# Streaming Conformer layer on one core: the last loads of x are tied behind weight casts, and 19 products by g move from GpSimd to VectorE

## The chip, the cores and the metric

The kernel runs on one core of one Trainium2 chip. The time is device microseconds of that core for one execution. The engines are TensorE (PE in the profile; PEld its weight loads), VectorE (DVE), ScalarE (ACT), GpSimd (POOL) and SyncE (SP), which here only starts transfers.

## The reference, cut to what matters

One layer is computed for 512 prompt frames and 64 sample frames (576 rows in all, width 2048). What the change touches is its end:

```python
mix = jnp.concatenate([conv_out * jax.nn.silu(cg), att * jax.nn.silu(ag), mem * jax.nn.silu(mg)], axis=-1)
y = layer_norm(ALPHA * x + mix @ w_out, ln_g, ln_b)
def layer_norm(x, g, b):
    mu = jnp.mean(xf, axis=-1, keepdims=True)
    var = jnp.mean(jnp.square(xf - mu), axis=-1, keepdims=True)
    return (xf - mu) * lax.rsqrt(var + LN_EPS) * g + b
```

All inputs are float32. The attention and memory half of `mix @ w_out` is finished earlier and waits in DRAM (`a_dram`); what is left for the end is the convolution half, of depth 1024.

## The kernel before, in words

**Weights.** A weight tile of 128x1024 is loaded by SP (`wraw`, line 175), or summed by a GpSimd transfer that adds to what is there (`w_add`, line 179). It is split in two: ScalarE casts it to the high part `whi` (line 248), VectorE subtracts that and gives the low part `wlo` (line 253). TensorE multiplies high by high, high by low and low by high. A pair `whi`, `wlo` is called a stage here; `next_stage` asks for it, and splits up to two stages ahead. All of `wraw`, `wsum`, `whi` and `wlo` share 14 buffers (`NW`), so a load or a cast also waits until the last reader of its buffer is done.

**The end of the kernel.** The output has four blocks of 512 columns, n = 0 to 3, and five row tiles, t = 0 to 4 (t = 4 are the 64 sample rows). Blocks 0 and 1 are computed together by `out_pair(0, ...)`, a scheme of seven products with two stages each: B11, T1, T2, B21, T3, B22 and T4 (stages 0 to 13), on TensorE in lines 1121 to 1127. The scheduler may reorder them: four matmuls of T2 and all of T3 wait for `t23l` of the last depth tile (line 1078), whose buffer is that of `xd`, and so TensorE does B22 and the `xd` matmuls of T4 (lines 1125 and 1127) ahead of them. Block 2 is a plain product of four stages (`tileB`, lines 343 to 349), block 3 another, written out in `part` row tile by row tile (lines 1405 to 1410).

**The tiles z.** z[t, n] holds ALPHA * x plus the attention half, then the sum with the convolution half. `load_z` starts the load of x on ScalarE's queue (line 1172); `form_z` scales it on ScalarE (line 1180) and starts a GpSimd transfer that adds `a_dram` to it (line 1181). For n = 2 and 3 `next_z(2)` does two tiles of each at a time, from stage 11 of `out_pair` on. VectorE adds the accumulators (lines 1361 and 1334) and takes statistics (lines 1366 and 1335); GpSimd multiplies z by g (lines 1367, 1337 and 1425; line 1430 does the last one on VectorE). `finish_stats` makes mean and rstd on GpSimd (lines 1300 to 1310), and `finish_pe` transposes them, lets TensorE form g times minus mean times rstd plus b (line 1323), and VectorE makes y (line 1326), which SP stores.

**Order.** A scheduler places the instructions of each engine by the order in the code and by its own estimate of when they can start; each engine then runs its list strictly in order. `tc.issue_after(ins)` makes the instructions of its block that run on the engine of `ins` stand behind `ins`.

Of the kernel before, what the change touches and what calls it, by code (L numbers as in the profile page):

```python
# [9 lines left out]
F32 = mybir.dt.float32  # L10
# [5 lines left out]
P = 128  # L16
NP_TOK = 512
NS_TOK = 64
# [110 lines left out]
def hymba_kernel(ctx: ExitStack, tc: tile.TileContext, wst, xT, memT, xp, xs, kcT, vc, mkcT, mvc, biasx,  # L129
                 cconvT, convw, convb, clg, clb, lngb, sel,  # L130
                 y_out, conv_out, kT_out, v_out, mkT_out, mv_out):
    nc = tc.nc
# [35 lines left out]
        return dpool.tile(shape, F32, tag=name, name=name)  # L168

    wraw, whi, wlo, sum3 = {}, {}, {}, {}  # L170

    def w_fetch(b):
        if b not in wraw:
            wraw[b] = wtile("wraw")
            nc.sync.dma_start(wraw[b], wst[where[b]])
        return wraw[b]
# [6 lines left out]
    def w_load(i):  # L183
        if i >= len(plan):
            return
        it = plan[i]
        if it[0] == "O":
            q = out_quads(*it[1:4])
            for b in item_blocks(it):
                w_fetch(b)  # L190
            if it in added:
                return
            added.add(it)
            if it[4] == "s1":
                w_add(w_fetch(q["a21"]), q["a22"])
            elif it[4] == "s3":
                sum3[it[1:4]] = wtile("wsum")
                nc.scalar.copy(sum3[it[1:4]], w_fetch(q["a11"]))
                w_add(sum3[it[1:4]], q["a21"])
            elif it[4] == "s4":  # L200
                w_add(w_fetch(q["a21"]), q["a12"])
            return
        for b in item_blocks(plan[i]):
            w_fetch(b)
        if plan[i][2:] == ("s1",) and plan[i][1] not in sum3:
            n = plan[i][1]
            q = quads(PAIRS[n])
            sum3[n] = wtile("wsum")
            nc.scalar.copy(sum3[n], w_fetch(q["a11"]))  # L209
            w_add(sum3[n], q["a21"])  # L210
            if n != 1:
                w_add(w_fetch(q["a21"]), q["a22"])

    def w_source(it):
        if it[0] == "P":
            return w_fetch(it[1])
        if it[0] == "O":
            q = out_quads(*it[1:4])
            if it[4][0] == "a":
                return w_fetch(q[it[4]])  # L220
            if it[4] == "s3":
                return sum3[it[1:4]]
            a21 = w_fetch(q["a21"])
            if it[4] == "s2":
                nc.vector.tensor_add(a21, a21, w_fetch(q["a11"]))
            return a21
        n, form = it[1:]
        q = quads(PAIRS[n])
        if form[0] == "a":
            return w_fetch(q[form])  # L230
        if form == "s3":
            return sum3[n]
        a21 = w_fetch(q["a21"])
        if form != "s1" or n == 1:
            nc.vector.tensor_add(a21, a21, w_fetch(q[{"s1": "a22", "s2": "a11", "s4": "a12"}[form]]))
        return a21
# [6 lines left out]
    def w_split(i):  # L243
        if i < len(plan) and i not in whi:
            w_load(i)
            src = w_source(plan[i])
            hi, lo = wtile("whi", F32R), wtile("wlo", F32R)
            nc.scalar.copy(hi, src)  # L248
            if by_transfer(i):
                nc.scalar.mul(lo, hi.bitcast(F32), -1.0)  # L250
                w_add(lo, plan[i][1])
            else:
                nc.vector.tensor_sub(lo, src, hi.bitcast(F32))  # L253
            whi[i], wlo[i] = hi, lo

    def weights(i):
# [63 lines left out]
    def tileB(lhs, tiles, sample, klist, ntaps=0, before=None, early=False, steps=2):  # L320
        accs = [bank("accB") for _ in tiles]
        sacc = bank("accS") if sample else None
        nk = len(klist)
        for s in range(nk // 2):
            if before:
                before(s)
            hi, lo = next_stage()
            for kk in range(2):
                ki = 2 * s + kk
                k = klist[ki]  # L330
                ws = slice(kk * 512, (kk + 1) * 512)
                st, en = ki == 0, ki == nk - 1
                if early and st:
                    for t, acc in zip(tiles, accs):
                        nc.tensor.matmul(acc, lhs(k, t)[0], hi[:, ws], start=True, stop=False)
                    for t, acc in zip(tiles, accs):
                        nc.tensor.matmul(acc, lhs(k, t)[0], lo[:, ws], start=False, stop=False)
                    for t, acc in zip(tiles, accs):
                        nc.tensor.matmul(acc, lhs(k, t)[1], hi[:, ws], start=False, stop=False)
                else:  # L340
                    for t, acc in zip(tiles, accs):
                        lh, ll = lhs(k, t)
                        nc.tensor.matmul(acc, lh, hi[:, ws], start=st, stop=False)  # L343
                        nc.tensor.matmul(acc, ll, hi[:, ws], start=False, stop=False)  # L344
                        nc.tensor.matmul(acc, lh, lo[:, ws], start=False, stop=en)  # L345
                if sample:
                    ss = sample(k)
                    nc.tensor.matmul(sacc, ss, hi[:, ws], start=st, stop=False)
                    nc.tensor.matmul(sacc, ss, lo[:, ws], start=False, stop=en)
            pump(ntaps, steps)  # L350
        return accs, sacc
# [810 lines left out]
    z = {}  # L1162

    zload = deque()

    def load_z(n, tiles=range(5)):

        for t in tiles:
            rows = P if t < 4 else NS_TOK
            ns = slice(n * 512, (n + 1) * 512)  # L1170
            z[t, n] = t5([P, 512], "z")
            nc.scalar.dma_start(z[t, n][:rows], xp[t * P:(t + 1) * P, ns] if t < 4 else xs[:, ns])
            zload.append((t, n))

    def form_z(count):

        for _ in range(min(count, len(zload))):
            t, n = zload.popleft()
            zt = z[t, n][:P if t < 4 else NS_TOK]
            nc.scalar.mul(zt, zt, ALPHA)  # L1180
            nc.gpsimd.dma_start(zt, a_dram[t, n][:P if t < 4 else NS_TOK], accum_op=ALU.add)
# [79 lines left out]
    for j in range(NCB):  # L1261
        if j + 3 < NCB:
            load_cg(j + 3)
        acc = tileA(srhs, 1)
# [17 lines left out]
    for n in range(4):  # L1282
        raw = t6([5, 512], "gbraw")
        nc.sync.dma_start(raw, lngb[:, n * 512:(n + 1) * 512])
        hi = t6([5, 512], "gbhi", F32R)
# [6 lines left out]
    def load_g(n):  # L1292
        g = t6([P, 512], "gb")
        nc.gpsimd.dma_start(g, lngb[0:1, n * 512:(n + 1) * 512].to_broadcast((P, 512)))
        return g
# [32 lines left out]
            return last  # L1328
        return [lambda n=n: apply(n)() for n in range(4)]

    def settle(t, n, acc, g, scaled=True):
        rows = P if t < 4 else NS_TOK
        zt = z[t, n][:rows]
        nc.vector.tensor_add(zt, out_source(t, acc), zt)
        nc.vector.bn_stats(stats[t][:rows, n], zt)
        if scaled:
            nc.gpsimd.tensor_mul(zt, zt, g[:rows])

    gpair = [load_g(n) for n in range(2)]

# [3 lines left out]

    ztiles = [(t, n) for n in (2, 3) for t in range(5)]

    def next_z(count):
        form_z(count)
        for _ in range(min(count, len(ztiles))):
            t, n = ztiles.pop(0)  # L1350
            load_z(n, (t,))

    def conv_forms(stage):
        if stage < 4:
            form234(stage, alloc_large)
        elif stage >= 11:
            next_z(2)

    def zsum(t, n, acc, op=None):
        zt = z[t, n][:P if t < 4 else NS_TOK]  # L1360
# [2 lines left out]
    def done(t, n):  # L1363
        rows = P if t < 4 else NS_TOK
        zt = z[t, n][:rows]
        nc.vector.bn_stats(stats[t][:rows, n], zt)
        nc.gpsimd.tensor_mul(zt, zt, gpair[n][:rows])

    def zsink(h, n, last, op=None):
        def f(acc):  # L1370
# [6 lines left out]
    def zsample(i, acc):  # L1377
# [5 lines left out]
    out_pair(0, {"p1": zsink(0, 0, False), "p5": zsink(1, 1, False, sub), "p16": zsink(1, 0, False),  # L1383
                 "p2": zsink(0, 0, True), "p167": zsink(1, 1, True, sub), "p53": zsink(1, 0, True),
                 "p1674": zsink(0, 1, True, sub), "sample": zsample}, conv_forms)
    g = load_g(2)
    accs, sacc = tileB(mlhs2, range(4), msl, list(range(8)), before=lambda s: next_z(2))
    while zload:
        next_z(2)
    g3 = load_g(3)  # L1390
    for t in range(4):
        settle(t, 2, accs[t], g)
    settle(4, 2, sacc, g)
    g = g3
    accs = [bank("accB") for _ in range(5)]

    def part(t, s, w):
# [16 lines left out]
    for t in (4, 0, 1, 2, 3):  # L1414
        todo = []
        for s in range(4):
            part(t, s, held[s])
            if due and (t > 0 and s == 3 and t < 4 or t == 1 and s == 2):
                todo += finish_pe(*due.pop(0))
        settle(t, 3, accs[t], g, False)  # L1420
        aggr, *rest = finish_stats(t)
        due.append((t, *rest))
        rows = P if t < 4 else NS_TOK
        if t != 3:
            nc.gpsimd.tensor_mul(z[t, 3][:rows], z[t, 3][:rows], g[:rows])
        with tc.issue_after(aggr.ins):
            for f in todo:
                f()
            if t == 3:
                nc.vector.tensor_mul(z[t, 3][:rows], z[t, 3][:rows], g[:rows])  # L1430
    for d in due:
        for f in finish_pe(*d):
            f()
# [69 lines left out]
```

## Time and profile before

| what | value |
|---|---|
| median of 3 runs | 954.44 us (950.99, 954.44, 955.18) |
| profiled execution, its own time | 950.69 us |
| its span, first to last instruction | 948.4 us |
| TensorE busy | 924.8 us, 98% of the span |
| VectorE busy | 740.7 us, 78% |
| ScalarE busy | 479.4 us, 51% |
| GpSimd busy | 149.5 us, 16% |

Each row group further down says which view it is from. A timeline row gives the start, the busy time, engine, line, operation and tiles; xN merges N like instructions, and the bracket at its end is the idle time of the engine ahead of it, and what ended it. Successive matmuls overlap in the record, so the step from one start to the next is the cost of one, not its duration.

### The profile page before, as it was taken

Reading aid. Unit: us, or ns where it says so; the run is one execution under the profiler, and the core shown is the slowest. Engines: PE = TensorE matmul, PEld = TensorE weight load, DVE = VectorE, ACT = ScalarE, POOL = GpSimd, SP = SyncE. Lnnn points to the kernel's source line nnn. Section 1 sums busy time; section 2 is a strip of 40 time slices with the busy share of each in tenths; the row PEclk is TensorE's granted clock in tenths of the full one; section 3 lists DMA queues with packets and bytes.
Section 4 is the critical chain, followed back from the end, with each engine's and each line's share of the span. In section 5 each row is a group of like instructions: output and inputs, shape, how many; then the busy total and the mean of one; then the engine's idle time right before and its main releaser. Section 6 shows DMA issues by size and latency. Waiting matters only on the chain. (4 is left out here: it accounts for less than half of the span.)

```text
span 948.4 us, 15430 instructions
## 1 busy us (share of the span) xinstructions
PE 924.8 (98%) x5965; PEld 852.3 (90%) x5965; DVE 740.7 (78%) x1072; ACT 479.4 (51%) x805; POOL 149.5 (16%) x217
## 2 busy tenths in 40 slices
PE   8999999999999999999999999999999999987996
PEld 5899999999999999999999988999888799965874
DVE  7878985997699699677999565279987886746766
ACT  6655444445444544464643556447756675533200
POOL 0020000100100110011110000200112212224452
PEclk9999999999999999999999999999999999997998
DMA  9746555655666766589867456974669688896305
GB/s 327 216 148 172 146 152 157 200 148 147 185 167 181 201 181 161 176 243 231 199 182 183 144 170 210 254 167 98 153 239 248 187 291 208 199 229 165 105 1 199
DMA packets 61771, 174.74 MB, mean 184 GB/s; under 512 B 7678, under 2 KB 12286, under 8 KB 61698
## 3 DMA queue, kind: packets, MB, share of 16 engines
q1 hardware_dynamic: 38834, 106.90, 34.2%
q0 software_dynamic: 16640, 54.62, 28.6%
q10 hardware_dynamic: 6224, 12.24, 3.8%
q8 instruction: 46, 0.75, 0.3%
q14 instruction: 27, 0.22, 0.1%
HBM read 150.40 MB, written 23.33 MB: 183 GB/s over the span
## 5 line engine op out<-in xcount | busy, mean ns | idle before, releaser
L248 ACT CAST whi<-wraw 128x1024 fp32r<-128x1024 f32 x195 | 203.6, 1049 | 177.2 <-PE st L559 51.4
L253 DVE TENSOR_TENSOR wlo<-wraw,whi 128x1024 fp32r<-128x1024 f32 x173 | 217.3, 1259 | 74.9 <-ACT whi L248 37.2
L559 PE MATMUL st<-x,whi 128*128 128x288 f32 x1024 | 204.6, 294 | 0.0
L519 DVE SCALAR_TENSOR_TENSOR acc<-up,cw_sb,acc 128x606 f32<-128x606 f32 x232 | 196.3, 846 | 4.2
L559 PEld LDWEIGHTS st<-x,whi 128*128 128x128 f32 x1024 | 164.0, 188 | 0.3 <-ACT neg L628 0.2
L559 PE MATMUL st<-x,wlo 128*128 128x288 f32 x512 | 150.8, 295 | 0.0
L315 PE MATMUL accA<-x,whi 128*128 128x288 f32 x768 | 134.9, 297 | 0.0
L315 PEld LDWEIGHTS accA<-x,whi 128*128 128x128 f32 x768 | 112.7, 189 | 1.6 <-issue 0.8
L559 PEld LDWEIGHTS st<-x,wlo 128*128 128x128 f32 x512 | 96.0, 188 | 0.0
L315 PE MATMUL accA<-x,wlo 128*128 128x288 f32 x384 | 82.2, 296 | 0.0
L559 PE MATMUL st<-t13h,wlo 128*128 128x288 f32 x256 | 75.5, 295 | 0.0
L559 PE MATMUL st<-t13l,whi 128*128 128x288 f32 x256 | 75.4, 295 | 0.0
L559 PE MATMUL st<-t13h,whi 128*128 128x288 f32 x256 | 75.4, 294 | 0.0
L1121 PE MATMUL ob<-whi,mix 128*128 128x512 f32 x176 | 58.0, 411 | 7.1 <-ACT whi L248 7.1
L315 PEld LDWEIGHTS accA<-x,wlo 128*128 128x128 f32 x384 | 61.8, 189 | 0.0
L179 POOL DMA_DIRECT2D wsum<-in_wst_dram x22 | 20.9, 950 | 216.8 <-ACT wsum L209 127.8
L559 PE MATMUL st<-t,whi 128*128 128x288 f32 x256 | 51.3, 295 | 0.0
L179 POOL DMA_DIRECT2D wraw<-in_wst_dram x27 | 27.0, 1012 | 137.7 <-DVE pos L615 57.4
L559 PEld LDWEIGHTS st<-t13h,whi 128*128 128x128 f32 x256 | 48.0, 188 | 0.0
L559 PEld LDWEIGHTS st<-t13l,whi 128*128 128x128 f32 x256 | 48.0, 188 | 0.0
L559 PEld LDWEIGHTS st<-t13h,wlo 128*128 128x128 f32 x256 | 48.0, 188 | 0.0
L1121 PEld LDWEIGHTS ob<-whi,mix 128*128 128x128 f32 x176 | 34.3, 199 | 15.0 <-ACT whi L248 7.9
(391 smaller groups left out, 1855.1 us busy)
## 6 DMA issues: line engine op xcount, KB each, us to landing
wraw<-in_wst_dram SPq DMA_DIRECT2D x151, 512.0 KB, 3.9
wraw<-in_wst_dram POOLq DMA_DIRECT2D x27, 512.0 KB, 7.2
wsum<-in_wst_dram POOLq DMA_DIRECT2D x22, 512.0 KB, 6.4
wlo<-in_wst_dram POOLq DMA_DIRECT2D x22, 512.0 KB, 7.6
xraw<-in_xT_dram SPq DMA_DIRECT2D x19, 288.0 KB, 5.9
ad<-c POOLq DMA_DIRECT2D x16, 256.0 KB, 5.1
z<-in_xp_dram ACTq DMA_DIRECT2D x16, 256.0 KB, 4.9
z<-ad POOLq DMA_DIRECT2D x16, 256.0 KB, 6.4
```

The costliest lines, as they stand in the source:

```text
L179: nc.gpsimd.dma_start(dst, wst[where[b]], accum_op=ALU.add)
L248: nc.scalar.copy(hi, src)
L253: nc.vector.tensor_sub(lo, src, hi.bitcast(F32))
L315: nc.tensor.matmul(acc[:, :HALF], stat[:, ws], mv[:, c], start=ki == 0 and pi == 0, stop=ki == len(klist) - 1 and pi == 2)
L519: nc.vector.scalar_tensor_tensor(acc[0], up[0][:, t:t + ACCW], cw_sb[:, j, t:t + 1], acc[0], op0=ALU.mult, op1=ALU.add)
L559: nc.tensor.matmul(acc[:, :HALF], stat[:, ws], mv, start=first and k == 0 and i == 0, stop=k == 7 and i == 2, skip_group_check=not first)
L1121: nc.tensor.matmul(a, stat[:, os_], mv[:, ws], start=first and ki == 0 and i == 0, stop=ki == 3 and i == 2, skip_group_check=not first)
```

## The change

It has three parts. `newest` remembers the last traced cast of a high part, and the last subtraction that made a low part. In `next_z` the scalings and loads of z for n = 2 and 3 stand behind the newest cast on ScalarE, and the first two calls only load, so that a scaling follows its load two calls later. The 10 products by g of blocks 0 and 1 are done on VectorE within block 2, behind low parts; the 9 others, of blocks 2 and 3, on VectorE within block 3, behind the statistics of a row tile. The diff, cut where it only renames:

```diff
@@ w_split @@
-            nc.scalar.copy(hi, src)
+            newest["cast"] = nc.scalar.copy(hi, src).ins
...
-                nc.vector.tensor_sub(lo, src, hi.bitcast(F32))
+                newest["low"] = nc.vector.tensor_sub(lo, src, hi.bitcast(F32)).ins
@@ settle, done @@
-        if scaled:
-            nc.gpsimd.tensor_mul(zt, zt, g[:rows])
...
-        nc.gpsimd.tensor_mul(zt, zt, gpair[n][:rows])
@@ next_z @@
-    def next_z(count):
-        form_z(count)
-        for _ in range(min(count, len(ztiles))):
-            t, n = ztiles.pop(0)
-            load_z(n, (t,))
+    def next_z(stage):
+        with tc.issue_after(newest["cast"]):
+            if stage > 1:
+                form_z(2)
+            for _ in range(min(2, len(ztiles))):
+                t, n = ztiles.pop(0)
+                load_z(n, (t,))
@@ conv_forms @@
         elif stage >= 11:
-            next_z(2)
+            next_z(stage - 11)
@@ block 2 @@
-    accs, sacc = tileB(mlhs2, range(4), msl, list(range(8)), before=lambda s: next_z(2))
-    while zload:
-        next_z(2)
+    def block2(s):
+        next_z(3 + s)
+        with tc.issue_after(newest["low"]):
+            for t, n in scale_g[3 * s:3 * s + 3]:
+                rows = P if t < 4 else NS_TOK
+                nc.vector.tensor_mul(z[t, n][:rows], z[t, n][:rows], gpair[n][:rows])
+    scale_g = [(t, n) for n in range(2) for t in range(5)]
+    accs, sacc = tileB(mlhs2, range(4), msl, list(range(8)), before=block2)
@@ block 3 @@
-        if t != 3:
-            nc.gpsimd.tensor_mul(z[t, 3][:rows], z[t, 3][:rows], g[:rows])
         with tc.issue_after(aggr.ins):
             for f in todo:
                 f()
-            if t == 3:
-                nc.vector.tensor_mul(z[t, 3][:rows], z[t, 3][:rows], g[:rows])
+            for u, n, g in [(t, 3, g3)] + [(u, 2, g2) for u in {4: (4, 0), 0: (1, 2, 3)}.get(t, ())]:
+                rows = P if u < 4 else NS_TOK
+                nc.vector.tensor_mul(z[u, n][:rows], z[u, n][:rows], g[:rows])
```

On ScalarE, from the high part of T2's second stage (`whi_9062`) on, this stood before; `whi_9084` and `whi_9101` are B21, `whi_9122` and `whi_9142` T3, `whi_9176` (in the changed kernel 9173) the first stage of B22, and the tiles z are those of blocks 2 and 3:

```order
L248 CAST whi_9062<-wraw_8832 128x1024 [waits PE_49]
L1172 DMA z_9238<-in_xp_dram 128x512 [waits DVE_49]
L1180 ACTIVATE z_9236<-z_9236 128x512 [waits DMAHW6_49]
L248 CAST whi_9084<-wraw_8983 128x1024 [waits DMAHW4_49,PE_49]
L1172 DMA z_9268<-in_xp_dram 128x512 [waits DMAHW0_49]
L1180 ACTIVATE z_9238<-z_9238 128x512 [waits DMAHW7_49]
L1172 DMA z_9270<-in_xp_dram 128x512 [waits DVE_49]
L248 CAST whi_9101<-wraw_9027 128x1024 [waits DMAHW5_49,DVE_49]
L1180 ACTIVATE z_9268<-z_9268 128x512 [waits DMAHW0_49]
L248 CAST whi_9122<-wsum_8985 128x1024 [waits DMASW5_49,PE_49]
L1180 ACTIVATE z_9270<-z_9270 128x512 [waits DMAHW1_49]
L248 CAST whi_9142<-wsum_9029 128x1024 [waits DMASW7_49,PE_49]
```

In the changed kernel the same engine has, from the second stage of T3 on (`whi_9173` and `whi_9191` are B22, `whi_9213` and `whi_9235` T4, `whi_9261` the first stage of block 2):

```order
L249 CAST whi_9142<-wsum_9029 128x1024 [waits DMASW7_49,PE_49]
L249 CAST whi_9173<-wraw_8766 128x1024 [waits DMASW6_49,DVE_49]
L249 CAST whi_9191<-wraw_8832 128x1024 [waits DMASW0_49,DVE_49]
L1159 COPY ztmp_9168<-os_1310_8931 64x512 [waits PE_49]
L249 CAST whi_9213<-wraw_9146 128x1024 [waits DMAHW6_49,PE_49]
L1173 DMA z_9231<-in_xp_dram 128x512
L1173 DMA z_9233<-in_xp_dram 128x512
L249 CAST whi_9235<-wraw_9177 128x1024 [waits DMAHW7_49,DVE_49]
L1173 DMA z_9257<-in_xp_dram 128x512
L1173 DMA z_9259<-in_xp_dram 128x512
L249 CAST whi_9261<-wraw_9195 128x1024 [waits DMAHW0_49,DVE_49]
L1181 ACTIVATE z_9231<-z_9231 128x512 [waits DMAHW1_49]
```

All loads and scalings of these tiles moved behind the casts of the first stage of T4 and later ones; the nine casts from `whi_9062` to `whi_9213` follow each other with nothing of z between them.

On SP the buffers fell otherwise, so that the weight loads wait for other instructions. Before, the four loads from the first stage of T4 (`wraw_9146`) to the second of block 2 (`wraw_9222`) read as follows; the DVE wait of the first is for the low part of T3's first stage:

```order
L175 DMA wraw_9146<-in_wst_dram 128x1024 [waits DMASW5_49,DMAHW3_49,DMASW1_49,DVE_49]
L175 DMA wraw_9180<-in_wst_dram 128x1024 [waits DMAHW6_49,PE_49]
L175 DMA wraw_9198<-in_wst_dram 128x1024 [waits DMAHW7_49,PE_49]
L175 DMA wraw_9222<-in_wst_dram 128x1024 [waits DMASW0_49,DMAHW0_49,DVE_49,Activation_49]
```

and in the changed kernel, where the PE waits of the first three are for the last matmul of T2's first stage, and for the last of B21's first and of its second stage:

```order
L176 DMA wraw_9146<-in_wst_dram 128x1024 [waits DMAHW6_49,DVE_49,PE_49]
L176 DMA wraw_9177<-in_wst_dram 128x1024 [waits DMAHW7_49,DVE_49,PE_49]
L176 DMA wraw_9195<-in_wst_dram 128x1024 [waits DMAHW0_49,DVE_49,PE_49]
L176 DMA wraw_9217<-in_wst_dram 128x1024 [waits DMASW0_49,DMAHW2_49,DVE_49,Activation_49]
```

The load of T4's first stage thus no longer waits for a low part that is made late in the chain, but for a matmul of T2.

On VectorE, within block 2, the low parts stood close together before (`wlo_9432` is the first of block 3):

```order
L1361 TENSOR_TENSOR z_8611<-z_8611,ob_1309_8930 128x512 [waits PE_49]
L1366 BN_STATS stats_8890<-z_8609 128x6 [waits DVE_49]
L1366 BN_STATS stats_8891<-z_8611 128x6 [waits DVE_49]
L253 TENSOR_TENSOR wlo_9432<-wraw_9306,whi_9431 128x1024 [waits DMAHW4_49,Activation_49]
L253 TENSOR_TENSOR wlo_9466<-wraw_9355,whi_9465 128x1024 [waits DMAHW6_49,PE_49,Activation_49]
```

and now have the products by g (`gb`) between them (`wlo_9341` and `wlo_9386` are the third and fourth stage of block 2, `wlo_9427` the first of block 3):

```order
L1369 BN_STATS stats_8891<-z_8611 128x6 [waits DVE_49]
L254 TENSOR_TENSOR wlo_9341<-wraw_9239,whi_9340 128x1024 [waits DMAHW5_49,Activation_49]
L1393 TENSOR_TENSOR z_8463<-z_8463,gb_8925 128x512
L1393 TENSOR_TENSOR z_8538<-z_8538,gb_8925 64x512
L1393 TENSOR_TENSOR z_8609<-z_8609,gb_8927 128x512 [waits DMASW1_49,DVE_49]
L254 TENSOR_TENSOR wlo_9386<-wraw_9265,whi_9385 128x1024 [waits DMAHW1_49,Activation_49]
L1393 TENSOR_TENSOR z_8611<-z_8611,gb_8927 128x512 [waits DVE_49]
L1393 TENSOR_TENSOR z_8685<-z_8685,gb_8927 128x512
L1393 TENSOR_TENSOR z_8687<-z_8687,gb_8927 128x512
L254 TENSOR_TENSOR wlo_9427<-wraw_9295,whi_9426 128x1024 [waits DMAHW2_49,DVE_49,Activation_49]
```

Ten products are new in this stretch of VectorE's list, three of them ahead of each of two low parts that TensorE needs within block 2 or at the start of block 3.

## Rows read from the trace of the kernel before

**Rows 1.** Windows of the end: start:end, length, busy (x) per engine, PEclk, DMA share, GB/s.
```profile
847.40:852.60 5.20, 4.64 (x12) 3.15 (x12) 3.62 (x5) 0.99 (x2) 0.82 (x1) 0.67 0.98 293
...
858.00:865.40 7.40, 5.60 (x13) 3.96 (x14) 5.77 (x6) 2.42 (x3) 3.89 (x4) 0.51 0.41 106
...
882.50:906.50 24.00, 24.00 (x106) 19.62 (x105) 14.15 (x13) 4.63 (x5) 7.33 (x7) 1.00 0.23 59
```

**Rows 2.** TensorE's timeline: last matmul of B21, first ones of B22, T4's end, block 3's start.
```profile
845.35 0.39 PE L1127 MATMUL os<-wlo,mixsamp 128*128 128x512 f32 x1
847.42 0.72 PE L1121 MATMUL ob<-whi,mix 128*128 128x512 f32 x2 [1.68 <-ACT whi L248]
...
858.00 2.07 PE L1121 MATMUL ob<-whi,mix 128*128 128x512 f32 x4 [5.39 <-ACT whi L248]
...
882.22 0.40 PE L1121 MATMUL ob<-wlo,t 128*128 128x512 f32 x1
...
906.39 0.39 PE L1409 MATMUL accB<-whi,mixsamp 128*128 128x512 f32 x1
```

**Rows 3.** Who waited for whom, 820 to 900 us: us in total, times, longest.
```profile
ACT z L1180 <- DMA z<-in_xp_dram: 17.9, 7, 4.2
...
PE ob L1121 <- ACT whi L248: 7.1, 2, 5.4
```

**Rows 4.** ScalarE's timeline around the casts of T3 and B22.
```profile
841.28 0.63 ACT L1180 ACTIVATE z<-z 128x512 f32<-128x512 f32 x1 [4.17 <-DMA z<-in_xp_dram]
...
856.38 0.63 ACT L1180 ACTIVATE z<-z 128x512 f32<-128x512 f32 x1 [3.51 <-DMA z<-in_xp_dram]
856.92 1.03 ACT L248 CAST whi<-wraw 128x1024 fp32r<-128x1024 f32 x1
857.85 0.58 ACT L1158 COPY ztmp<-os 64x512 f32<-64x512 f32 x1
```

**Rows 5.** Transfers issued at 828 to 832 and 832 to 836: KB, us to landing.
```profile
wsum<-in_wst_dram POOLq DMA_DIRECT2D x1, 512.0 KB, 7.3
wraw<-in_wst_dram POOLq DMA_DIRECT2D x1, 512.0 KB, 8.9
z<-in_xp_dram ACTq DMA_DIRECT2D x2, 256.0 KB, 9.6
z<-ad POOLq DMA_DIRECT2D x2, 256.0 KB, 9.0
```

**Rows 6.** Weight loads of SP issued at 844 to 848.
```profile
wraw<-in_wst_dram SPq DMA_DIRECT2D x3, 512.0 KB, 8.7
```

**Rows 7.** VectorE's timeline: low parts, sums, statistics, the waits in block 3.
```profile
842.89 1.23 DVE L253 TENSOR_TENSOR wlo<-wsum,whi 128x1024 fp32r<-128x1024 f32 x1 [4.52 <-ACT whi L248]
...
848.54 1.28 DVE L1361 TENSOR_TENSOR z<-z,ob 128x512 f32<-128x512 f32 x2
849.74 1.28 DVE L1366 BATCH_NORM_STATS2 stats<-z 128x6 f32<-128x512 f32 x2
...
859.07 2.75 DVE L253 TENSOR_TENSOR wlo<-wraw,whi 128x1024 fp32r<-128x1024 f32 x1
...
885.08 5.44 DVE L253 TENSOR_TENSOR wlo<-wraw,whi 128x1024 fp32r<-128x1024 f32 x1
...
915.65 0.69 DVE L1334 TENSOR_TENSOR z<-accB,z 128x512 f32<-128x512 f32 x1 [1.25 <-PE accB L1407]
...
921.48 0.69 DVE L1334 TENSOR_TENSOR z<-accB,z 128x512 f32<-128x512 f32 x1 [4.11 <-PE accB L1407]
...
941.43 0.69 DVE L1430 TENSOR_TENSOR z<-z,gb 128x512 f32<-128x512 f32 x1
```

**Rows 8.** GpSimd's timeline: an issue beside a low part, two issues, two products.
```profile
842.21 0.89 POOL L1181 DMA_DIRECT2D z<-ad  x1 [5.72 <-ACT z L1180]
...
885.11 1.75 POOL L1181 DMA_DIRECT2D z<-ad  x2
886.27 3.16 POOL L1367 TENSOR_TENSOR z<-z,gb 128x512 f32<-128x512 f32 x2
```

More of the change, by code (lines that the diff above doesn't have):

```diff
@@ L170, in hymba_kernel @@
     wraw, whi, wlo, sum3 = {}, {}, {}, {}
+    newest = {}
     def w_fetch(b):
@@ L1329, in finish_pe, with settle @@
         return [lambda n=n: apply(n)() for n in range(4)]
-    def settle(t, n, acc, g, scaled=True):
+    def settle(t, n, acc):
         rows = P if t < 4 else NS_TOK
@@ L1385, in hymba_kernel @@
                  "p1674": zsink(0, 1, True, sub), "sample": zsample}, conv_forms)
-    g = load_g(2)
-    accs, sacc = tileB(mlhs2, range(4), msl, list(range(8)), before=lambda s: next_z(2))
-    while zload:
-        next_z(2)
+    def block2(s):
[5 more added lines that the diff above has]
+    scale_g = [(t, n) for n in range(2) for t in range(5)]
+    g2 = load_g(2)
+    accs, sacc = tileB(mlhs2, range(4), msl, list(range(8)), before=block2)
     g3 = load_g(3)
     for t in range(4):
-        settle(t, 2, accs[t], g)
-    settle(4, 2, sacc, g)
-    g = g3
+        settle(t, 2, accs[t])
+    settle(4, 2, sacc)
     accs = [bank("accB") for _ in range(5)]
@@ L1419, in hymba_kernel @@
                 todo += finish_pe(*due.pop(0))
-        settle(t, 3, accs[t], g, False)
+        settle(t, 3, accs[t])
         aggr, *rest = finish_stats(t)
         due.append((t, *rest))
-        rows = P if t < 4 else NS_TOK
-        if t != 3:
-            nc.gpsimd.tensor_mul(z[t, 3][:rows], z[t, 3][:rows], g[:rows])
         with tc.issue_after(aggr.ins):
```

## The prediction

> **What bounds the kernel now.** The page's first two parts come first: TensorE is busy for 98% of the span, so only a stretch where it waits, or runs at less than its full clock, can give much. The slices show one such stretch ahead of the very end, near 840 to 880 us. The view by windows sizes it: the granted clock falls to 0.67 and then to 0.51, which is the 1.2 GHz level, while from 882.5 on it is back at 1.00 and 106 matmuls take 24.0 us, 0.226 us each [rows 1]. TensorE's timeline gives the ends of the bad stretch: B21's last matmul starts at 845.35, so the product ends at 845.6; T4's last starts at 882.22 and ends at 882.4; and block 3 begins at 906.4 [rows 2]. Between 845.6 and 882.4 it has to do 24 matmuls of B22, 8 with `xd`, 4 left of T2, 24 of T3, 24 of T4 and a few of block 2. As the changed kernel orders them that is 90, or 20.3 us at 0.226. It takes 36.8. So 16.5 us are lost there, and that is the most that the change can win here.
>
> The view of waits says why: TensorE waited for high parts from ScalarE, 7.1 us in two waits, and ScalarE, ahead of its scalings of z, for loads of x, 17.9 us in seven [rows 3]. ScalarE's timeline joins the two: a scaling that ends a wait of 4.17 us at 841.3, another that ends one of 3.51 us at 856.4, and the cast that TensorE needs right behind it [rows 4]. TensorE's longest wait, 5.39 us, ends with that cast, and the next one, the 1.2 GHz matmuls and the late low parts follow from it [rows 2].
>
> **Loads and scalings tied behind casts.** Nothing is removed: ten loads, ten scalings and ten adding transfers are moved later. The casts from T2's second stage to T4's first then wait only for data, buffers and VectorE. I walk the changed order with prices from the rows: matmul 0.226, high part 1.03, copy 0.58, low part 1.23, and 0.64 for a sum or statistics [rows 1, 4, 7].
>
> Up to 845.6 TensorE never waited, so it gains nothing there. Are B22's pairs ready? The last sum for T3 was issued before 832 and took 7.3 us, so it is there by 839.3; high and low part make 841.6; B22's first pair takes 2.3 more, 843.9; the second's data, issued before 836 with 8.9, is there by 844.9 [rows 5], its high part at 845.9. These are upper bounds, since four loads of x no longer share the DMA engines, and both high parts are in time.
>
> 1. B22, first stage: 12 matmuls, 845.6 to 848.3.
> 2. VectorE has two sums, two statistics and the sample's sum (5 x 0.64) to do after B21 and ahead of B22's second low part: 845.6 + 3.2 + 1.23 = 850.0. TensorE does four high products until 849.2, waits 0.8, and ends B22 at 851.8.
> 3. One sum and T4's first low part: 851.9. That frees the buffer for the second high part, 852.9, its low part 854.2. TensorE waits 0.1 and then some 1.2 us, and the `xd` matmuls end at 854.9.
> 4. `t23l` takes 0.64, until 855.5; the wait is 0.4 with one matmul of block 2 in it. The rest of T2 and two of block 2 end at 856.9, T3 (24) at 862.3, its sums being 0.64 behind and covered by three matmuls of block 2, and T4 at 868.4.
>
> **Sum.** T4 ends at 868.4 and not at 882.4: 14.0 us of the 16.5 come back, and 2.5 stay as short waits. From there both kernels have 106 matmuls of block 2.
>
> The loads of T4 and block 2 must hold that pace. T4's first was queued on SP behind a low part of T3 that ScalarE's waits made late; now it waits for T2's first stage, over at 845.6 less 40 matmuls (32 of B21, 8 of T2), 836.6. The next two wait for the halves of B21, 842.0 and 845.6. At the 8.7 us that three issued together took [rows 6] they land at 850.7 and 854.3; they are wanted at 851.9 and 854.2. That costs nothing or 0.1, and at shorter landings nothing.
>
> **Where the stall goes.** The scalings now stand ahead of the second high part of block 2. With the longest landing seen, 9.6 us [rows 5], the first pair, issued by 850, is scaled by 861; the high part is wanted at 868.4 + 22 x 0.226 = 873.4. The last tile of block 2's z is loaded behind that scaling: 861 + 9.6 + 0.63 + 0.9 to issue + 9.0 to land [rows 5, 8] = 881, and the sum that reads it comes at 892.4. So 11 us remain; for block 3 no less. This is the cover of the move, and it is priced below.
>
> **19 products to VectorE.** Each costs 0.69 on VectorE [rows 7]; 19 make 13 us of work there. Ten fall into block 2. Its third low part comes after four sums and statistics behind T4, 868.4 + 4 x 0.64 + 1.23 = 872.2; the fourth three products later, 875.5; block 3's first after three more, 878.8. TensorE wants them at 868.4 + 50 x 0.226 = 879.7, at 886.0 and at 892.4, so at least 7.5 us cover them. Nine fall into block 3: three behind the sample's statistics where VectorE idled 1.25 us, four where it idled 4.11 [rows 7], two more behind y. The first three, 2.1 us, are 0.8 too long by that count, but the sums ahead no longer meet a GpSimd product. I take 0. If the cover is gone, row tile 0 is 0.8 later.
>
> What GpSimd loses is worth more than its time. Low parts beside its products took 2.75 and 5.44 us instead of 1.23 [rows 7, 8]; the first, at 859, was waited for. The walk has it at 1.23 already, so no extra term is added. An adding transfer's issue alone (842.2) left the low part at 842.9 at 1.23, but two issues and two products together stand beside the 5.44, which the rows can't split. Bounds for an issue beside VectorE: 0 and its own 0.9 [rows 7, 8]. I take 0, for the row where it stands alone.
>
> **Totals.** 948.4 - 14.0 = 934.4 for the span; with the 2.3 around it 936.7 for an execution like the profiled one (950.69). The runs shown lie near 951 twice (the profiled one among them) and near 955 twice, and their median is 954.44; I add half of that difference, 1.9, for I can't tell which kind the next median falls on: 938.6.
>
> **The rivals.**
>
> *The clock falls again.* The walk leaves 2.5 us of waits between 849 and 855.5. Before, a wait of 1.68 us and a short one behind it [rows 2] were followed by the fall to 0.67: 12 matmuls took 4.64 instead of 2.7, 1.9 lost; in the window at 0.51, 13 took 5.60 instead of 2.9, 2.7 lost [rows 1]. One such fall gives 940.5 to 941.3, two some 943.2. For it: the waits lie close together. Against: none is above 1.2 us. Chance 0.20.
>
> *VectorE stays stretched.* The ten adding issues stay on GpSimd, and VectorE has more work beside them. At 0.9 each, two of them on the path give 940.4; if it is as bad as the 5.44 (4.2 too much) twice, 947.0. For it: the unsplit row. Against: the row at 842. The Trainium skill's page "GPSIMD Engine Reference", section "Key points", has GpSimd share its SBUF interfaces with VectorE, with contention for instructions with two SBUF inputs, as low parts and these products are. By that rule a product by g on VectorE is itself exposed wherever GpSimd still touches SBUF; the trace agrees for products beside products (5.44), and no row here shows it for an issue alone. Chance 0.12.
>
> *The edge moves the wait only.* ScalarE still stops at the scalings, so a pair of loads that lands 12 us after the longest landing seen makes block 2's second high part late, and 26 us after it nothing of the 14 us is left: 938.6 + 14.0 = 952.6. Against: the DMA share was 0.98 at 847 to 852 but 0.41 at 858 to 865 [rows 1], so there is room behind. Chance 0.03.
>
> *Slower: z comes too late.* The sums of block 2 wait for the last adding transfer. Due at 881 by the slow walk, it costs from 892.4 on: each us late is one of VectorE's list, on which y hangs. At 906.4, 25 us behind the slow walk, the gain is used up (952.6), and at 912 the kernel ends at 958. For it: the scalings now stand two calls behind their loads, so the transfers start later against the sums than they did. Against: five transfers would each have to take 6 us more, one after the other. Chance 0.03.
>
> **How the numbers follow.** The forecast has 0.62, with 938.6 and, by the two kinds of run, 936.7 to 940.5; were the 2.5 us of waits to vanish too, 934.2. The clock reaches 943.2, VectorE 947.0. The range from 934 to 946 leaves out the last two rivals (0.06), the worst of VectorE and some unseen gain. About 0.5% (4.8 us) is what a measurement of this kernel tells from no change. Forecast, clock and nearly all of VectorE lie below 949.7, 0.93 for faster; the moved wait and VectorE beyond its bound are within 0.5%, 0.04; slower 0.03.
>
> **What would show it.** In the changed profile: no load of x ends a wait of ScalarE ahead of a cast of T3, B22 or T4; B21's end to T4's end takes some 23 us and not 36.8; the clock is 1.00 or has one short dip there; low parts are at 1.23 and GpSimd has no products left; block 2 and block 3 keep their lengths. The prediction is wrong if TensorE still waits several us for high parts in B22, if SP's loads land after them, or if a sum in block 2 or 3 waits for an adding transfer.

## The result, and the profile after

The changed kernel takes 938.2 us (median of 4 runs, 935.82 to 939.56) against 952.72 us for the kernel before (4 runs, 950.67 to 955.18): a ratio of 0.984, 95% interval 0.981 to 0.988. The profiled execution took 935.82 us. On another chip later it took 937.0 against 953.1, 0.983 (0.981 to 0.985).

The page of the changed kernel, its span, the busy times and the granted clock by slices:

```profile
span 934.0 us, 15429 instructions
...
PE 919.6 (98%) x5965; PEld 849.9 (91%) x5965; DVE 743.0 (80%) x1091; ACT 478.9 (51%) x805; POOL 122.2 (13%) x198
...
PEclk9999999999999999999999999999999999999998
```

The span is 14.4 us shorter, and the clock row has no dip left ahead of the last slice. The windows of the same kernel that answer to [rows 1], and the stretch from B21's end to T4's end as a whole:

```profile
845.20:867.70 22.50, 21.64 (x92) 16.71 (x91) 20.10 (x29) 11.05 (x15) 6.48 (x9) 1.00 0.92 270
...
847.40:852.60 5.20, 4.73 (x21) 3.51 (x19) 4.69 (x6) 2.10 (x2) 0.00 (x0) 1.00 0.81 278
...
858.00:865.40 7.40, 7.40 (x35) 6.11 (x34) 7.40 (x12) 4.21 (x6) 3.56 (x4) 1.00 1.03 292
...
867.70:891.70 24.00, 24.00 (x106) 19.63 (x105) 15.13 (x21) 5.87 (x7) 3.55 (x5) 1.00 0.59 143
```

Where 12 and 13 matmuls were done at a clock of 0.67 and 0.51, 21 and 35 are done at 1.00. TensorE's timeline, to be read beside [rows 2]:

```profile
845.00 0.40 PE L1128 MATMUL os<-wlo,mixsamp 128*128 128x512 f32 x1
...
852.70 0.50 PE L1128 MATMUL os<-wlo,xd 128*128 128x512 f32 x1 [0.58 <-DVE wlo L254]
...
854.45 0.50 PE L1122 MATMUL ob<-whi,t23l 128*128 128x512 f32 x1 [0.17 <-DVE t23l L1079]
...
867.43 0.40 PE L1122 MATMUL ob<-wlo,t 128*128 128x512 f32 x1
...
892.06 0.39 PE L1416 MATMUL accB<-whi,mixsamp 128*128 128x512 f32 x1
```

From the start of B21's last matmul to that of T4's last it is 22.43 us, against 36.87 before [rows 2]: 14.4 us. The two waits of 0.58 and 0.17 us are all that TensorE's matmul rows name there; its weight loads (PEld) name some more. Who waited for whom from 820 to 886 us (compare [rows 3]):

```profile
ACT z L1181 <- DMA z<-in_xp_dram: 4.6, 2, 2.3
...
PE os L1128 <- DVE wlo L254: 0.6, 1, 0.6
PEld accB L344 <- ACT whi L249: 0.6, 1, 0.6
...
PE ob L1122 <- DVE t23l L1079: 0.2, 1, 0.2
```

ScalarE waits for loads of x of the prompt rows in two places instead of seven, 4.6 us instead of 17.9 (for those of the sample rows it waits once in either kernel, 1.2 us and 1.4 before). No matmul waits for a high part any more; one weight load does, of block 2, for 0.6 us, and the step to its matmul (853.27 to 853.78) is 0.3 us longer for it. ScalarE's timeline shows where the scalings went (compare [rows 4]):

```profile
847.99 1.05 ACT L249 CAST whi<-wraw 128x1024 fp32r<-128x1024 f32 x1 [1.98 <-PE ob L1122]
848.00 0.82 ACTq L1173 DMA_DIRECT2D z<-in_xp_dram  x2
850.34 1.05 ACT L249 CAST whi<-wraw 128x1024 fp32r<-128x1024 f32 x1 [1.30 <-DVE wlo L254]
...
852.68 1.05 ACT L249 CAST whi<-wraw 128x1024 fp32r<-128x1024 f32 x1 [1.29 <-DVE wlo L254]
...
853.63 1.15 ACT L1181 ACTIVATE z<-z 128x512 f32<-128x512 f32 x2
...
858.79 1.05 ACT L249 CAST whi<-wraw 128x1024 fp32r<-128x1024 f32 x1 [3.54 <-PE ob L1122]
...
869.46 0.63 ACT L1181 ACTIVATE z<-z 128x512 f32<-128x512 f32 x1 [2.23 <-DMA z<-in_xp_dram]
```

The first pair of loads is issued at 848.0 with two casts behind it, and when its scalings are reached at 853.6 it has landed. From T2's second stage to T4's first there are eight casts, not the nine that the section on the change counts, and nothing of z stands between them. All casts of B22 to T4 wait for low parts or for matmuls; the first scaling that still waits stands at 869.5, ahead of a cast that has time.

VectorE's timeline (compare [rows 7]) has the low parts at their length and the products in their new places:

```profile
847.36 1.21 DVE L254 TENSOR_TENSOR wlo<-wraw,whi 128x1024 fp32r<-128x1024 f32 x1
...
858.82 2.34 DVE L254 TENSOR_TENSOR wlo<-wraw,whi 128x1024 fp32r<-128x1024 f32 x2
...
864.13 0.67 DVE L1393 TENSOR_TENSOR z<-z,gb 128x512 f32<-128x512 f32 x1
...
870.79 1.88 DVE L1393 TENSOR_TENSOR z<-z,gb 128x512 f32<-128x512 f32 x3
...
889.72 1.38 DVE L1335 TENSOR_TENSOR z<-accB,z 128x512 f32<-128x512 f32 x2 [7.80 <-PE accB L346]
...
907.15 0.69 DVE L1335 TENSOR_TENSOR z<-accB,z 128x512 f32<-128x512 f32 x1 [1.77 <-PE accB L1414]
```

The row at 858.82 holds two low parts that overlap in the record, of 1.21 and 1.22 us. GpSimd has no product by g left. Its timeline has issues of adding transfers (compare [rows 8]) and, in block 3, the small operations of the statistics:

```profile
860.67 1.80 POOL L1182 DMA_DIRECT2D z<-ad  x2 [3.21 <-ACT z L1181]
863.38 1.75 POOL L1182 DMA_DIRECT2D z<-ad  x2 [0.91 <-ACT z L1181]
...
903.71 0.89 POOL L1307 TENSOR_TENSOR lnmv<-lnmv,mhalf 128x1 f32<-128x1 f32 x1
904.68 0.76 POOL L1308 TENSOR_TENSOR lnmv<-lnmv 128x1 f32<-128x1 f32 x1
...
909.22 0.56 POOL L1307 TENSOR_TENSOR lnmv<-lnmv,mhalf 128x1 f32<-128x1 f32 x1
909.85 0.19 POOL L1308 TENSOR_TENSOR lnmv<-lnmv 128x1 f32<-128x1 f32 x1
```

### The profile page after: what moved, and what is told of

It reads as the page before. It is cut to its first block, busy times and chain, and to the rows that moved or that the text cites. A ratio compares the mean times of both kernels' runs of the same rounds, so it can differ in the third digit from the quotient of the medians.

```text
span 934.0 us, 15429 instructions
## 1 busy us (share of the span) xinstructions
PE 919.6 (98%) x5965; PEld 849.9 (91%) x5965; DVE 743.0 (80%) x1091; ACT 478.9 (51%) x805; POOL 122.2 (13%) x198
## 5 line engine op out<-in xcount | busy, mean ns | idle before, releaser
L254 DVE TENSOR_TENSOR wlo<-wraw,whi 128x1024 fp32r<-128x1024 f32 x173 | 210.1, 1219 | 72.9 <-ACT whi L249 31.2
L1122 PE MATMUL ob<-whi,mix 128*128 128x512 f32 x176 | 55.3, 394 | 0.0
L236 DVE TENSOR_TENSOR wraw<-wraw,wraw 128x1024 f32<-128x1024 f32 x33 | 40.2, 1217 | 6.9 <-DMA wraw<-in_wst_dram 6.7
```

Source lines behind the costliest of these rows:

```text
L254: newest["low"] = nc.vector.tensor_sub(lo, src, hi.bitcast(F32)).ins
L1122: nc.tensor.matmul(a, stat[:, os_], mv[:, ws], start=first and ki == 0 and i == 0, stop=ki == 3 and i == 2, skip_group_check=not first)
```

## The experiments

The theory: TensorE lost its 16.5 us because ScalarE, which works its list in order, stopped ahead of casts at scalings that waited for loads of x; the products' move adds only what GpSimd's products cost low parts that TensorE waits for. Rival 1: the gain is the products' move. Rival 2: the early loads of x delayed the weights' transfers, and their later place is the gain. All runs in one table. "Stretch" is from the start of B21's last matmul to that of T4's last in the profiled execution; the ratio is to the kernel before on the same chip.

| kernel | median us (runs) | ratio, 95% interval | stretch us |
|---|---|---|---|
| before (three chips) | 951.9, 952.8, 953.1 | 1 | 36.9 |
| changed, again | 937.0 (4) | 0.983, 0.981 to 0.985 | 22.5 |
| ties only | 941.5 (4) | 0.988, 0.985 to 0.991 | 26.0 |
| products only | 949.9 (10) | 0.998, 0.995 to 1.000 | 33.7 |
| scalings tied, loads early | 936.8 (4) | 0.984, 0.980 to 0.988 | 22.5 |
| scalings one call earlier | 937.2 (4) | 0.985, 0.981 to 0.989 | 23.1 |
| first ten products on GpSimd | 940.2 (4) | 0.985, 0.980 to 0.989 | 27.3 |
| last nine products on GpSimd | 936.8 (4) | 0.981, 0.975 to 0.986 | 22.5 |
| all five calls earlier, distance one | 946.2 (7) | 0.992, 0.989 to 0.995 | 31.3 |
| all five calls earlier, distance two | 943.8 (4) | 0.988, 0.983 to 0.993 | 29.3 |
| scalings tied, ten products | 938.0 (5) | 0.985, 0.982 to 0.987 | 22.5 |

**Each part alone.** *Ties only:* the kernel before with the new `next_z`.

```diff
+        with tc.issue_after(newest["cast"]):
+            if stage > 1:
+                form_z(2)
+            for _ in range(min(2, len(ztiles))):
...
+            next_z(stage - 11)
...
+    accs, sacc = tileB(mlhs2, range(4), msl, list(range(8)), before=lambda s: next_z(3 + s))
```

> The kernel before with the loads and scalings of x tied behind casts; all products by g stay where they were, 18 of 19 on GpSimd. Theory (TensorE lost its 16.5 us because ScalarE, ahead of casts, stopped at scalings that waited for loads of x): B21's end to T4's end takes 22 to 26 us and not 36.8, no load of x ends a wait of ScalarE ahead of a cast of T3 or B22, and the time is 938 to 942 us, a ratio of 0.983 to 0.988; what it lies above the changed kernel, 0 to 3 us, is the products' share. Rival 1 (the gain came from taking GpSimd's products away from beside the low parts): at most 3 us gained, 950 us or more. Rival 2 (the loads' traffic delayed the weights): as the theory, since the loads move too.

It is 19 products of 20 that stay on GpSimd here; the twentieth was on VectorE already.

*Products only:* the changed kernel with the old `next_z(2)`.

```diff
-        with tc.issue_after(newest["cast"]):
-            if stage > 1:
-                form_z(2)
+        form_z(count)
```

> The changed kernel with loads and scalings of x where the kernel before had them; all 19 products on VectorE. Theory: ScalarE still waits some 18 us for loads of x between 820 and 885, TensorE still waits about 7 us for high parts, and the time is 948 to 953 us: the gain is 0 to 4 us, all of it from low parts that take 1.23 us where two took 2.75 and 5.44. Rival 1 (products): 936 to 942 us. Rival 2: as the theory.

Ties alone shorten the stretch by 10.9 us, products alone by 3.2, both by 14.4: in the profiled executions the two parts nearly add up. By the medians they give 10.4 and 2.0 us against 14.5 for both; the runs with products only lie too far apart (946.3 to 953.8) to say whether the parts help each other. Rival 1 falls. In the kernel with products only the waits from 820 to 900 us are of the same kind as in [rows 3] and of a like size:

```profile
ACT z L1181 <- DMA z<-in_xp_dram: 22.6, 7, 4.9
...
PE ob L1122 <- ACT whi L249: 6.4, 2, 4.5
```

In the kernel with ties only, ScalarE no longer stops ahead of a cast of T3 to T4, but VectorE's timeline shows low parts, and a sum with both sources in SBUF, that are stretched beside GpSimd's products (846.71 to 850.24, 852.61 to 853.88 and 860.70 to 864.24):

```profile
849.01 1.78 DVE L1366 TENSOR_TENSOR z<-z,ztmp 64x512 f32<-64x512 f32 x1
...
853.03 1.92 DVE L254 TENSOR_TENSOR wlo<-wraw,whi 128x1024 fp32r<-128x1024 f32 x1 [0.51 <-ACT whi L249]
...
861.12 4.20 DVE L254 TENSOR_TENSOR wlo<-wraw,whi 128x1024 fp32r<-128x1024 f32 x2
```

The sum takes 1.78 us and not 0.68, so the low part that follows is 1.1 late; its successor takes 0.7 too long, two more 1.9 together. TensorE's timeline of this kernel pays for them:

```profile
855.01 0.50 PE L1128 MATMUL os<-wlo,xd 128*128 128x512 f32 x1 [1.46 <-DVE wlo L254]
...
865.97 0.73 PE L1122 MATMUL ob<-whi,t 128*128 128x512 f32 x2 [1.25 <-DVE z L1366]
```

**Which products.** The changed kernel with the first ten products back on GpSimd, and with the last nine there:

```diff
-            for t, n in scale_g[3 * s:3 * s + 3]:
...
+        nc.gpsimd.tensor_mul(zt, zt, gpair[n][:rows])
```

> The changed kernel with the ten products by g of output blocks 0 and 1 back on GpSimd, behind their statistics, and the nine of blocks 2 and 3 on VectorE. Ties only took 941.5 us, 3 us above the changed kernel, and showed low parts of 1.92, 4.20 (two) and 4.19 us beside GpSimd products between 853 and 879. Theory (the share of the products is what GpSimd costs low parts in the stretch of B22, T3 and T4): nearly all of the 3 us comes back, 940 to 942.5 us. Rival (the products of blocks 2 and 3 cost it, at the end): as the changed kernel, 936 to 939.5 us.

```diff
+        if scaled:
+            nc.gpsimd.tensor_mul(zt, zt, g[:rows])
...
+        if t != 3:
+            nc.gpsimd.tensor_mul(z[t, 3][:rows], z[t, 3][:rows], g[:rows])
```

> The reverse: the ten products of blocks 0 and 1 on VectorE, those of blocks 2 and 3 on GpSimd as in the kernel before (the last one on VectorE). Theory: as the changed kernel, 936 to 939.5 us, since no low part that is waited for stands beside them. Rival: 940 to 942.5 us.

The first ten hold all of the products' share, 3.4 us between the two medians; where the last nine are done makes no difference that a median shows. The windows of the kernel with the first ten on GpSimd show that part of its 27.3 us of stretch is the clock:

```profile
853.00:856.00 3.00, 1.55 (x4) 1.12 (x4) 1.40 (x1) 1.57 (x3) 0.31 (x1) 0.72 0.84 308
856.00:859.00 3.00, 2.64 (x7) 1.73 (x6) 1.39 (x3) 0.99 (x3) 2.69 (x4) 0.50 0.65 161
```

Some 15 matmuls from 854.45 on step at 0.43 us instead of 0.23, which by estimate is 3 us. Ahead of that the waits on `xd` low parts were 0.39 and 1.46 us, practically those of the kernel with ties only (0.40 and 1.46), where the same windows were granted 1.00:

```profile
853.00:856.00 3.00, 1.46 (x4) 0.67 (x4) 1.92 (x1) 1.01 (x3) 0.87 (x1) 1.00 0.93 326
856.00:859.00 3.00, 2.74 (x10) 1.85 (x11) 2.16 (x4) 1.56 (x4) 2.13 (x4) 1.00 0.67 167
```

That kernel's stretch is 26.0 us at full clock, 3.5 more than the changed kernel's, so the stretched low parts cost that much without any fall of the clock. How much of the 3.4 us between the medians is the clock is not shown.

**The loads' traffic.** Only the scalings stay tied; the loads go out early again.

```diff
-        with tc.issue_after(newest["cast"]):
-            if stage > 1:
+        if stage > 1:
+            with tc.issue_after(newest["cast"]):
                 form_z(2)
```

> The changed kernel, but only the scalings stay behind their casts; the loads of x are issued as early as in the kernel before. Theory (the stop of ScalarE is what counted): within 2 us of the changed kernel, 936 to 941 us, B21's end to T4's end 22 to 25 us. Rival 2 (the loads' transfers delayed those of the weights): the waits for weights come back and the time is 945 to 953 us. Where the loads land before their scalings are reached, z is ready sooner than in the changed kernel, which has no use for that.

The loads are issued from 827.6 on, as in the kernel before, and the stretch is 22.5 us. Rival 2 falls. The traffic does delay a weight, though: ScalarE's timeline has the cast of T3's second stage behind a wait for its data, 2.15 us later than in the changed kernel (836.13), and TensorE has no wait that follows from it:

```profile
838.28 1.06 ACT L249 CAST whi<-wsum 128x1024 fp32r<-128x1024 f32 x1 [2.89 <-DMA wsum<-in_wst_dram]
```

**How far behind its load a scaling has to stand.** First one call instead of two, in the place of the changed kernel:

```diff
-            if stage > 1:
+            if stage > 0:
```

> The changed kernel with the scalings one call behind their loads and not two, still tied behind casts: the first pair now stands ahead of the cast of T4's first stage or the one after it. Theory: that cast waits until the pair loaded near 848 to 851 has landed, some 4 to 9 us after its issue, so ScalarE shows a wait for a load of x ahead of a cast again, TensorE a wait of 1 to 4 us for a high part or low part behind it, and the time is 939 to 943 us. If only the loads' place mattered and not the scalings' distance from them: as the changed kernel, 936 to 940 us.

This expectation of the theory missed: 937.2 us, as the changed kernel. The stops are there, 12.9 us for loads of x in six waits, but ScalarE's timeline shows what they hit:

```profile
856.62 0.64 ACT L1181 ACTIVATE z<-z 128x512 f32<-128x512 f32 x1 [2.21 <-DMA z<-in_xp_dram]
...
859.25 0.63 ACT L1181 ACTIVATE z<-z 128x512 f32<-128x512 f32 x1 [1.99 <-DMA z<-in_xp_dram]
...
860.26 1.05 ACT L249 CAST whi<-wraw 128x1024 fp32r<-128x1024 f32 x1
```

In the changed kernel ScalarE waits 3.54 us there for TensorE in any case, and its cast stands at 858.79. Two stops of 4.2 us in all, where the changed kernel has the same two scalings, move it by 1.5 us, of which 0.5 lies ahead of B21's end already, and the stretch grows by 0.7, which the median doesn't show. That fits a stop that costs only what it exceeds the engine's own idle time ahead of that cast, 4.2 less 3.54 us. If that is so, the same stops must cost in the stretch of B21 and B22. The next two kernels begin loads and scalings five calls earlier, at distances of one call and of two:

```diff
-        elif stage >= 11:
-            next_z(stage - 11)
+        elif stage >= 6:
+            next_z(stage - 6)
```

> The changed kernel with loads and scalings of x begun five calls earlier, still tied behind casts, and each scaling one call behind its load. The scalings of the first four pairs now stand ahead of the casts of B21's end, T2, B22 and T3 instead of T4 and block 2. Theory (what costs is a stop ahead of casts that TensorE is about to need): ScalarE waits some 4 to 9 us per pair less the 2.3 to 4.4 us between two casts, 8 to 18 us in all, TensorE waits 4 to 7 us for high parts, and the time is 944 to 952 us. If ties behind casts were what helped, wherever they are: 936 to 940 us.

> As the run before it, but each scaling two calls behind its load as in the changed kernel. Loads and their traffic lie in the same place as in the run before; only the scalings move one cast on. Theory: with two casts, some 5 to 7 us, between load and scaling most of the landing is covered, stops of ScalarE of 0 to 4 us per pair are left and the time is 937 to 945 us, at least 3 us below the run before. Rival (the traffic of the early loads delays the weights): as the run before, within 2 us.

They lose 9.1 and 6.8 us against the changed kernel (937.0, on another chip), or 9.4 and 7.0 against the 936.8 of the kernel with the last nine products on GpSimd on their own chip. At distance one ScalarE waits 16.9 us for loads of x of the prompt rows, and TensorE 5.4 for a high part of B22. Ties behind casts thus don't bring the gain wherever they are; the two kernels still lie 3.7 and 6.1 us below products only (949.9, another chip). The second lies 2.4 us below the first, where the theory wanted 3 and the rival under 2; the runs of the two overlap, so the times don't decide it, but the kernel with early loads and late scalings had already spoken against the traffic. Two calls are no safe distance here because casts follow closely: loads issued behind a cast at 837.1 were due for scaling two casts later, and still waited until 843.9. The timelines of the kernel at distance two, ScalarE:

```profile
852.21 0.63 ACT L1181 ACTIVATE z<-z 128x512 f32<-128x512 f32 x1 [2.04 <-DMA z<-in_xp_dram]
852.74 0.57 ACT L1159 COPY ztmp<-os 64x512 f32<-64x512 f32 x1
```

then VectorE:

```profile
853.34 0.68 DVE L1160 TENSOR_TENSOR ztmp<-os,ztmp 64x512 f32<-64x512 f32 x1 [3.08 <-ACT ztmp L1159]
853.95 1.20 DVE L254 TENSOR_TENSOR wlo<-wraw,whi 128x1024 fp32r<-128x1024 f32 x1
```

and TensorE:

```profile
855.21 0.73 PE L1122 MATMUL ob<-wlo,mix 128*128 128x512 f32 x2 [3.77 <-DVE wlo L254]
```

The stop reaches TensorE by a detour: it holds the copy of the sample's output, VectorE's list waits for that copy, and behind it stands the low part of B22, whose high part had been cast at 848.2. The granted clock then fell to 0.66 (855 to 860 us); in the kernel at distance one it fell to 0.53 behind a wait of 5.4.

**The least that is needed.** Scalings tied, loads early, ten products on VectorE and nine on GpSimd, beside the changed kernel unaltered:

```diff
-        with tc.issue_after(newest["cast"]):
-            if stage > 1:
+        if stage > 1:
+            with tc.issue_after(newest["cast"]):
                 form_z(2)
...
+        if scaled:
+            nc.gpsimd.tensor_mul(zt, zt, g[:rows])
```

> The least that the runs so far leave as needed: the scalings of x tied two calls behind, as in the changed kernel, the loads left early as in the kernel before, the ten products of blocks 0 and 1 on VectorE and the nine others on GpSimd. Theory (these two parts hold all of the gain): 936 to 939 us, within 1 us of the changed kernel run beside it. If the loads' tie or the last nine products are worth something only together: 939 to 942 us.

> The changed kernel unaltered, beside the run before on one chip: 936 to 940 us, as timed first (938.2). It shows whether the leaner kernel differs from it by more than 1 us.

938.0 (936.0 to 941.5) and 937.0 (935.9 to 937.8) can't be told apart. The gain is in two of the edits: scalings behind casts, and ten products off GpSimd. No kernel tried lies below the changed one by more than its runs scatter.

## Why the prediction was right

It gave 938.6 us, and 938.2 were measured; the span was put at 934.4, and it is 934.0.

- **The loss and what comes back.** B21's end to T4's end was forecast as 22.8 us (845.6 to 868.4), 20.3 of them matmuls and 2.5 waits. It is 22.4, so 2.1 are lost. The waits lie where the walk had them but are shorter: `xd` 0.58 and not 1.3, `t23l` 0.17 and not 0.4, and none for B22's second low part, which was put at 850.0 and done by 848.6. The walk lined up five sums and statistics behind B21's end; two of them began at 844.3, beside its last matmuls. The other 1.3 us are mostly gaps of 0.1 to 0.3 us to which the matmul rows give no cause; the largest stand behind weight loads that waited for a low part (1.0 us), a high part (0.6), `t23l` (0.5) and a sum (0.3).
- **The 1.9 us for the noise.** An execution like the profiled one was put at 936.7 and took 935.8; half the difference of two kinds of run, 1.9, was added to meet the median. The changed kernel's runs show no two kinds (935.8, 937.6, 938.8, 939.6), and on the other chip the profiled execution (937.64) lies above its median (937.04). That the median came within 0.4 us of the forecast is therefore in part luck; the 14.0 us forecast against 14.4 measured is not.
- **Block 2.** "From there both kernels have 106 matmuls of block 2" was off by two: T4's last matmul to block 3's first takes 24.6 us and not 24.2. B21 ends 0.35 us earlier, where no gain was expected. The two cancel, and block 3 begins 14.3 us earlier.
- **SP's loads.** Forecast to start at 836.6, 842.0 and 845.6; they start at 836.4, 841.8 and 845.4, and the casts at 850.34 and 852.68 wait for low parts, not for them. The cost of nothing holds. Nor is their earlier start the gain: the high part that TensorE waited 5.39 us for before was B22's second, whose data came by GpSimd's queue, issued at 832.2 and landed by 841.1 [rows 5], and was cast at 856.92 behind the stop [rows 4].
- **The z cover.** The first pair was allowed until 861 and is scaled at 853.6 to 854.8. The first sum of block 2 waits 7.80 us for TensorE and not for an adding transfer. In the kernel with the scalings one call earlier, a stop of 5.6 us within block 2 costs nothing that the median shows.
- **The products.** Low parts forecast to end by 872.2, 875.5 and 878.8 end at 870.9, 873.8 and 876.8; VectorE still idles 0.57 us ahead of row tile 0's sum, where the prediction counted 0.8 too long, and 1.77 ahead of row tile 1's. Zero was right, shown by the kernel with the last nine on GpSimd. What the prediction did not say is how much of its 14.0 us hung on the low parts' 1.23 us: with GpSimd's products left in place 3.4 to 4.7 us of it are missing (first ten on GpSimd, 940.2, and ties only, 941.5, each against the 936.8 of a kernel with the ten on VectorE on its own chip), part of it perhaps by the clock.
- **The issues.** Taken as 0, with 0.9 each as the bound. The row that the prediction went by is weak: the issue at 842.21 ends at 843.10 and the low part beside it begins at 842.89, so the two share 0.2 us. The changed kernel has better ones: the product at 864.13 and most of the sum of two SBUF tiles at 864.73 stand beside the issues from 863.38 to 865.13, and keep 0.67 us. The zero holds, no low part of its end is stretched, and the rival that VectorE stays stretched falls. The rows still don't put all of the 5.44 us of [rows 7] down to products: those beside it begin at 886.27 [rows 8], 1.19 us after the low part, which takes 1.2 us alone, and the product ahead ended at 885.17. In the kernel with ties only a low part at 874.84 takes 4.19 us, beside issues from 874.83 on and a product from 875.97 on only. What held these two ahead of the products is open.
- **The clock.** No fall in the changed kernel. That the rival was no empty one is shown by the two kernels with the same waits of 0.4 and 1.46 us: in one the clock fell to 1.2 GHz, in the other it stayed at 2.4. What decided between them is open. The changed kernel's waits are shorter, 0.58 and 0.17, and neither of its two profiled executions has a fall there; how long a wait may be, no run shows.
- **The other rivals.** That the wait only moves, and that z comes too late, fell with the rows above.

## What to carry to other kernels

An operation that waits for a transfer belongs behind the operations that the busiest engine waits for, at a distance that is longer than the landing in time and not in count of instructions; and by the one place measured here, a stop costs only what it exceeds the idle time that the engine has there anyway. Look at the lists of other engines too: here a stop of ScalarE reached TensorE by a copy that VectorE waited for. Of work that is moved off GpSimd, only that counted here which stood beside operations that were waited for.

## What was not expected of the hardware

**GpSimd's products stretch VectorE only where both sources lie in SBUF.** VectorE's timeline of the kernel with the last nine on GpSimd:

```profile
892.24 1.27 DVE L1335 TENSOR_TENSOR z<-accB,z 128x512 f32<-128x512 f32 x2
...
897.52 1.60 DVE L1335 TENSOR_TENSOR z<-ztmp,z 64x512 f32<-64x512 f32 x1
```

and GpSimd's, beside them:

```profile
891.83 6.75 POOL L1338 TENSOR_TENSOR z<-z,gb 128x512 f32<-128x512 f32 x5 [13.82 <-DVE stats L1336]
```

Two sums that read `accB`, a bank of PSUM, keep their 0.64 us each beside five products; the sum of two SBUF tiles takes 1.60 instead of 0.68, and another at 895.32 takes 0.85. In no run is a sum with a source in PSUM longer beside a product (0.66 to 0.69 us) than without one. The Trainium skill's page "GPSIMD Engine Reference", section "Key points", names contention for VectorE instructions with two SBUF inputs; these rows agree, and show sums with one source in PSUM that go without it.

**The contention works in both directions, down to one column.** Two sources in SBUF don't mean that VectorE is the one to be stretched. In the kernel before, two low parts, at 879.82 and 881.56, keep their length, and the three products beside them take 2.4 us each instead of 1.28; VectorE, then GpSimd:

```profile
879.82 1.21 DVE L253 TENSOR_TENSOR wlo<-wraw,whi 128x1024 fp32r<-128x1024 f32 x1
878.06 7.11 POOL L1367 TENSOR_TENSOR z<-z,gb 128x512 f32<-128x512 f32 x3 [0.73 <-DVE stats L1366]
```

In the changed kernel's rows of GpSimd above, the operations at 903.71 and 904.68 take 0.89 and 0.76 us, and the same two at 909.22 and 909.85 take 0.56 and 0.19. The first two stand beside four products by g on VectorE (from 902.96 to 905.39), the last two do not. The repeat on another chip has the same 0.89 and 0.76, and the kernel with the last nine on GpSimd 0.56 and 0.19 throughout. The statistics of row tile 0 come about 1.2 us later by it, which nothing waited for here.
